# Attention logits with the high query part multiplied into both key parts at once, kept in the outputs' PSUM banks, and softmax weights normalized by ScalarE

## The chip, the cores and the metric

One core of one Trainium2 chip runs the whole program. The metric is device time in microseconds (us) of one execution. The kernel before takes 2760.2 us (median of 3 runs, 2759.58 to 2760.26).

## The reference

The program is a two-layer decoder trunk on 256 tokens of width 2048, all in float32. Layer 0 is retention plus an MLP plus a gated per-layer embedding; layer 1 is block-sparse attention plus the same two. One attention block holds 256 keys, so with 256 tokens every query sees only its own block, causally, and the attention of layer 1 is plain causal softmax attention of 16 heads of width 128 with a relative-position bias:

```
l = einsum('hqd,hkd->hqk', q, k) * dh ** -0.5
l = where(dist >= 0, l + bias[:, bucket(dist)], NEG_INF)
p = softmax(l, axis=-1)
out = einsum('hqk,hkd->hqd', p, v) @ w_o
```

Keys and values come from the normalized stream after layer 0.

## The kernel before

**Arithmetic.** Every float32 operand is cut into a high part (a cast to fp32r on ScalarE, line 221) and a low part (the difference, on VectorE, line 222), and a product is the sum of three matmuls: high by high, high by low, low by high. This goes for weights and activations alike.

**Units.** All weights are streamed as units of 128x1024. A list of units is worked off in order by `run` (line 105): for unit i it issues the load of a pair of units (line 93, on SyncE's queue), splits unit i+3 into `wh` and `wl` (`conv`, line 96; `LOOK` is 3 and there are 4 buffers of each), issues unit i's matmuls, and then runs the tasks that were registered for i. So the order of the instructions on each engine is the order in which this loop writes them; nothing is rearranged later.

**Attention.** The 16 heads are worked in four groups of four (`attention`, line 709). A group has 24 units: 8 for the keys (`ak`), 8 for the queries (`aq`, two per head), 8 for the values (`av`). In a key or query unit TensorE does 8 matmuls of 512 columns (line 155) and 8 of 256 (line 153); in a value unit 12 of 512 (lines 195 to 197). With b the group's first unit, the tasks are:

- after the second query unit of head j (b+9+2j): the two halves of the query's PSUM bank are added (`fold`: ScalarE line 226, VectorE line 227) into `qt`; one unit later `qt` is split into high and low part, `qx` (lines 221 and 222, lines 746 to 752).
- `logits(j)` at b+11+2j (line 757): six matmuls into one bank of the tag `aux` (2 banks), per head: for the first 128 queries against 128 keys, then for the second 128 queries against 256 keys. Then VectorE scales and adds the bias table (line 773), takes the row maximum (line 774), ScalarE does the exponential with the row sum (line 775), VectorE takes the reciprocal (line 776) and multiplies the weights by it (line 779).
- `turn(j)` at b+15+2j: three transposes of the weights (line 786), split into `ph_` and `pl_`.
- `values(j)` at b+25+j//2, in the next group's first units: the weights times the values, in a bank of the tag `y` (2 banks), split into the outputs `o`.

So between the logits of head j and those of head j+1 lie two units, and on VectorE the order is: logits work of head j, `wl` of one unit, low part of `qx` of head j+1, `wl` of the next unit, `fold` of head j+2, logits work of head j+1.

Of the kernel before, what the change touches and what calls it, by code (L numbers as in the profile page):

```python
# [13 lines left out]
AF = mybir.ActivationFunctionType  # L14
ALU = mybir.AluOpType
AX = mybir.AxisListType

P = 128
S = 256
# [51 lines left out]
class Core:  # L71
# [637 lines left out]
    def attention(self):  # L709
        nc = self.nc  # L710
        mm = nc.tensor.matmul
        first = len(self.units)
        self.at(first + 4, self.stats_a)
        self.at(first + 6, self.stats_b)
        sc = {}

        def q_scale():
            sc["s"] = self.cp.tile([P, 2], F32, name="qs")
            nc.vector.tensor_scalar_mul(sc["s"], self.rn, DH ** -0.5)
        self.at(first + 8, q_scale)  # L720
        self.ot = {}
        for g in range(AH // GH):
            b, st = len(self.units), {}

            def table(st=st, g=g):
                st["T"] = []
                bv = self.io["bvec"]
                for j in range(0, GH, 2):
                    t = self.slot("T", (P, 2, S))
                    for q in range(0, P, BR):  # L730
                        src = bass.AP(tensor=bv.tensor, offset=bv.offset + (g * GH + j) * BR * 384 + 127 - q, ap=[[383, BR], [BR * 384, 2], [1, S]])
                        nc.sync.dma_start(t[q:q + BR], src)
                    st["T"] += [t[:, 0], t[:, 1]]
            self.at(b, table)

            def evac_k(n, ps, st=st):
                t = self.small("kt")
                self.fold(t, ps)
                yield
                yield  # L740
                nc.vector.tensor_mul(t, t, self.rb)
                x = self.slot("kx", dt=F32R)
                self.split(x[:, :S], x[:, S:], t)
                st["k", n] = x

            def evac_q(n, ps, st=st):
                t = self.small("qt")
                self.fold(t, ps)
                yield
                x = self.slot("qx", dt=F32R)  # L750
                self.split(x[:, :S], x[:, S:], t)
                st["q", n] = x

            self.phase_a(f"ak{g}_", "att", g * 24, GH, 2, LEAD if g == 0 else 1, lambda k: self.xx[k], evac_k)
            self.phase_a(f"aq{g}_", "att", g * 24 + 8, GH, 2, 1, lambda k: self.x2[k], evac_q)

            def logits(j, st=st):
                ps = self.aux("lg")
                q, k = st["q", j], st["k", j]
                for t in range(2):  # L760
                    o = ps[:, :P] if t == 0 else ps[:, P:384]
                    n = P * (t + 1)
                    qh, ql = q[:, t * P:(t + 1) * P], q[:, S + t * P:S + (t + 1) * P]
                    mm(o, qh, k[:, :n], start=True, stop=False)
                    mm(o, qh, k[:, S:S + n], start=False, stop=False)
                    mm(o, ql, k[:, :n], start=False, stop=True)
                l = self.slot("lg", (P, 384))
                mx = self.cp.tile([P, 2], F32, name="mx", tag="mx", bufs=2)
                sm = self.cp.tile([P, 2], F32, name="sm", tag="sm", bufs=2)
                for t in range(2):  # L770
                    c = slice(0, P) if t == 0 else slice(P, 384)
                    bias = st["T"][j][:, P:] if t == 0 else st["T"][j]
                    nc.vector.scalar_tensor_tensor(l[:, c], ps[:, c], sc["s"][:, t:t + 1], bias, op0=ALU.mult, op1=ALU.add)
                    nc.vector.reduce_max(mx[:, t:t + 1], l[:, c], axis=AX.X, negate=True)
                    nc.scalar.activation(l[:, c], l[:, c], AF.Exp, bias=mx[:, t:t + 1], accum_out=sm[:, t:t + 1])
                nc.vector.reciprocal(sm, sm)
                for t in range(2):
                    c = slice(0, P) if t == 0 else slice(P, 384)
                    nc.vector.tensor_scalar_mul(l[:, c], l[:, c], sm[:, t:t + 1])
                st["p", j] = l  # L780

            def turn(j, st=st):
                p = st.pop(("p", j))
                ps = self.aux("pt")
                for i, (c, o) in enumerate(((0, 0), (1, 1), (2, 2))):
                    nc.tensor.transpose(ps[:, o * P:(o + 1) * P], p[:, c * P:(c + 1) * P], self.ident)
                h, l = self.slot("ph_", (P, 384), F32R), self.slot("pl_", (P, 384), F32R)
                self.split(h, l, ps[:, :384])
                st["t", j] = (h, l)

            def evac_v(banks, st=st):
                st["v"] = self.natural(banks, self.rn)

            def values(j, st=st, g=g):
                (vh, vl), (ph, pl) = st["v"], st["t", j]
                ps = self.bank("y", "y", 2)
                c = slice(j * P, (j + 1) * P)
                for t in range(2):
                    o = ps[:, :S] if t == 0 else ps[:, P:S]
                    p = slice(0, S) if t == 0 else slice(S, 384)  # L800
                    mm(o, vh[t][:, c], ph[:, p], start=t == 0, stop=False)
                    mm(o, vh[t][:, c], pl[:, p], start=False, stop=False)
                    mm(o, vl[t][:, c], ph[:, p], start=False, stop=t == 1)
                x = self.slot(f"o{g}_{j}", dt=F32R)
                self.split(x[:, :S], x[:, S:], ps[:, :S])
                self.ot[g * GH + j] = x

            self.phase_b(f"av{g}_", "att", g * 24 + 16, KD // 2, lambda k: self.xx[k], evac_v)
            for j in range(GH):
                self.at(b + 11 + 2 * j, lambda j=j, f=logits: f(j))  # L810
                self.at(b + 15 + 2 * j, lambda j=j, f=turn: f(j))
                self.at(b + 25 + j // 2, lambda j=j, f=values: f(j))

        self.project("att_o", "att_o", 0, KD // 2, lambda k: self.ot[k], self.add([G_MLP1]))
# [82 lines left out]
```

## Time and profile before

| | |
|---|---|
| median of 3 runs | 2760.2 us |
| profiled execution, its own time | 2760.45 us |
| span of the profiled execution | 2758.6 us |
| TensorE busy | 2745.0 us, 13776 matmuls |
| VectorE busy | 1687.8 us |
| ScalarE busy | 1316.7 us |
| granted TensorE clock | 0.999 of full speed |
| HBM traffic | 189 GB/s over the span |

The span is what the trace covers; the execution's own time is 1.85 us longer. The durations below are from this one execution. A matmul's start is observed and its end is modelled, so the distance between starts is what a matmul takes of TensorE.

### The profile page before, as it was taken

The page shows a single profiled execution, that of the slowest core. Times are in us where ns is not written, and L with a number is a line of the kernel's source. Part 1 is how long each engine was busy: PE and PEld are TensorE (multiplying, and loading weights), DVE is VectorE, ACT ScalarE, POOL GpSimd, SP SyncE. Part 2 cuts the span into 40 slices and gives each one's busy share as a digit, 9 for nine tenths or more (in the row PEclk, how much of TensorE's full clock was granted, in tenths as well). Part 3 has the DMA queues.
Part 4 walks back from the last instruction along what each step waited for, and adds up shares of the span by engine and source line. Part 5 has one row for each costly group of instructions (what it writes and reads, how often), then busy time and mean ns, then how long its engine had stood idle before and what let it go on. Part 6 is the DMA issues. An engine that isn't in the chain of part 4 may idle for free.

```text
span 2758.6 us, 34142 instructions
## 1 busy us (share of the span) xinstructions
PE 2745.0 (100%) x13776; PEld 2336.5 (85%) x13776; DVE 1687.8 (61%) x2289; ACT 1316.7 (48%) x1812; POOL 0.2 (0%) x4
## 2 busy tenths in 40 slices
PE   9999999999999999999999999999999999999998
PEld 7888888888888888888888888888888888888886
DVE  6766666655576545665546766665666446664555
ACT  6444444444454433554446555555544334544454
POOL 0000000000000000000000000000000000000000
PEclk9999999999999999999999999999999999999999
DMA  7455555555555555555565555554555555555554
GB/s 278 176 186 186 186 186 186 186 183 189 185 191 190 192 198 188 194 184 197 185 201 193 179 187 179 176 183 177 189 187 195 193 190 196 185 191 190 186 200 153
DMA packets 79451, 522.50 MB, mean 189 GB/s; under 512 B 8987, under 2 KB 12988, under 8 KB 17596
## 3 DMA queue, kind: packets, MB, share of 16 engines
q1 hardware_dynamic: 78476, 519.20, 52.7%
q10 hardware_dynamic: 816, 1.11, 0.3%
q8 instruction: 108, 1.77, 0.3%
q14 instruction: 51, 0.42, 0.0%
HBM read 517.39 MB, written 2.88 MB: 189 GB/s over the span
## 4 chain that ended last, share of the span: by engine, by line
PE 99%; DMA 0%; DVE 0%; ACT 0%; issue 0%; SPq 0%
PE up L155 17%; PE up L153 9%; PE qk L155 4%; PE ak L155 2%; PE aq L155 2%; PE qk L153 2%; PE ak L153 1%; PE aq L153 1%; PE pu L573 1%; PE xt L255 1%; PE y L461 1%; PE qk L182 0%; PE dn__11046 L195 0%; PE dn__11047 L196 0%; PE dn__21304 L197 0%; PE dn__20701 L196 0%
## 5 line engine op out<-in xcount | busy, mean ns | idle before, releaser
L222 DVE TENSOR_TENSOR wl<-raw,wh 128x1024 fp32r<-128x1024 f32 (+1 forms) x971 | 1180.0, 1221 | 656.8 <-ACT wh L221 643.8
L221 ACT CAST wh<-raw 128x1024 fp32r<-128x1024 f32 (+1 forms) x971 | 1014.9, 1050 | 714.0 <-DVE rs_y L278 29.2
L155 PE MATMUL up<-x,wh 128*128 128x512 f32 x2048 | 490.5, 391 | 0.0
L155 PEld LDWEIGHTS up<-x,wh 128*128 128x128 f32 x2048 | 376.0, 188 | 72.5
L153 PEld LDWEIGHTS up<-x,wl 128*128 128x128 f32 x2048 | 263.4, 191 | 10.4
L153 PE MATMUL up<-x,wl 128*128 128x256 f32 x2048 | 266.6, 283 | 0.0
L226 ACT COPY t<-up 128x256 f32<-128x256 f32 x128 | 47.7, 373 | 331.7 <-PE up L155 331.7
L227 DVE TENSOR_TENSOR t<-t,up 128x256 f32<-128x256 f32 x128 | 53.9, 421 | 217.0 <-ACT t L226 216.9
L155 PE MATMUL qk<-x,wh 128*128 128x512 f32 x448 | 109.9, 392 | 0.0
L155 PEld LDWEIGHTS qk<-x,wh 128*128 128x128 f32 x448 | 81.8, 188 | 15.5
L233 ACT ACTIVATE x<-xt,g 128x256 fp32r<-128x256 f32 x112 | 52.6, 479 | 51.1 <-DVE x L234 39.5
L234 DVE SCALAR_TENSOR_TENSOR x<-xt,g,x 128x256 fp32r<-128x256 f32 x112 | 53.0, 481 | 26.2 <-ACT x L233 26.0
L155 PE MATMUL aq<-x,wh 128*128 128x512 f32 x256 | 63.2, 391 | 0.0
L155 PE MATMUL ak<-x,wh 128*128 128x512 f32 x256 | 63.1, 392 | 0.0
L153 PEld LDWEIGHTS qk<-x,wl 128*128 128x128 f32 x448 | 57.4, 191 | 2.2
L153 PE MATMUL qk<-x,wl 128*128 128x256 f32 x448 | 58.1, 283 | 0.0
L533 DVE SCALAR_TENSOR_TENSOR s<-t 128x256 f32<-128x256 f32 x128 | 54.3, 425 | 4.4
L155 PEld LDWEIGHTS ak<-x,wh 128*128 128x128 f32 x256 | 46.6, 188 | 8.8
L155 PEld LDWEIGHTS aq<-x,wh 128*128 128x128 f32 x256 | 46.5, 188 | 8.7
L222 DVE TENSOR_TENSOR a<-s,a 128x256 fp32r<-128x256 f32 x128 | 53.6, 419 | 0.0
L221 ACT CAST a<-s 128x256 fp32r<-128x256 f32 x128 | 52.1, 407 | 0.0
L242 ACT ACTIVATE sq<-h 128x512 f32<-128x512 f32 x48 | 30.1, 628 | 37.4 <-DVE h L542 15.6
(1011 smaller groups left out, 4991.4 us busy)
## 6 DMA issues: line engine op xcount, KB each, us to landing
raw<-mlp_up SPq DMA_DIRECT2D x128, 1024.0 KB, 4.8
raw<-mlp_dn SPq DMA_DIRECT2D x128, 1024.0 KB, 4.8
raw<-ret_in SPq DMA_DIRECT2D x94, 1024.0 KB, 4.8
raw<-att SPq DMA_DIRECT2D x48, 1024.0 KB, 4.8
raw<-ret_out SPq DMA_DIRECT2D x32, 1024.0 KB, 4.7
raw<-ple_gate SPq DMA_DIRECT2D x32, 1024.0 KB, 4.8
raw<-att_o SPq DMA_DIRECT2D x16, 1024.0 KB, 4.8
raw<-ple_up SPq DMA_DIRECT2D x4, 1024.0 KB, 4.8
```

What stands on the lines that cost most here:

```text
L153: mm(ps[:, S:], wl[:, c], rhs[k][:, :S], start=False, stop=end)
L155: mm(ps, wh[:, c], rhs[k], start=first and k == 0, stop=end)
L221: self.nc.scalar.copy(dst_h, src)
L222: self.nc.vector.tensor_sub(dst_l, src, dst_h.bitcast(F32))
L226: self.nc.scalar.copy(dst, ps[:, :S])
L227: self.nc.vector.tensor_add(dst, dst, ps[:, S:])
L233: self.nc.scalar.activation(t[:, :S], src, AF.Copy, scale=gs)
L234: self.nc.vector.scalar_tensor_tensor(t[:, S:], src, gs, t[:, :S].bitcast(F32), op0=ALU.mult, op1=ALU.subtract)
L242: self.nc.scalar.activation(self.slot("sq"), self.h[c][:, t], AF.Square, accum_out=self.ssq[:, t, c:c + 1])
L255: self.nc.tensor.transpose(ps[:, o * P:(o + 1) * P], self.h[c][:, t, f * P:(f + 1) * P], self.ident)
L461: mm(ys[t], a, w, start=i == 0, stop=i == len(ops) - 1)
L533: nc.vector.scalar_tensor_tensor(s, t, 0.0, t, op0=ALU.max, op1=ALU.mult)
```

## The change

Three things change, all in `logits`:

- Per 128 queries there are two matmuls instead of three. The high part of the queries is multiplied with the high and the low part of the keys side by side, in one matmul of 256 columns (first 128 queries) or 512 (second 128 queries); the low part of the queries is then added onto the first half. The two halves are not summed in PSUM any more.
- The results lie in two banks of the tag `y`, one per 128 queries, instead of one bank of the tag `aux`.
- VectorE scales and adds twice per 128 queries: the first half with the bias, then the second half onto that. The multiplication of the weights by the reciprocal row sum moves from VectorE to ScalarE.

```diff
             def logits(j, st=st):
-                ps = self.aux("lg")
                 q, k = st["q", j], st["k", j]
-                for t in range(2):
-                    o = ps[:, :P] if t == 0 else ps[:, P:384]
-                    n = P * (t + 1)
+                pss = []
+                for t in range(2):
+                    ps, n = self.bank("lg", "y", 2), P * (t + 1)
                     qh, ql = q[:, t * P:(t + 1) * P], q[:, S + t * P:S + (t + 1) * P]
-                    mm(o, qh, k[:, :n], start=True, stop=False)
-                    mm(o, qh, k[:, S:S + n], start=False, stop=False)
-                    mm(o, ql, k[:, :n], start=False, stop=True)
+                    x = k if t else k.rearrange("p (a s) -> p a s", a=2)[:, :, :P]
+                    o = ps if t else ps[:, :S].rearrange("p (a s) -> p a s", a=2)
+                    mm(o, qh, x, start=True, stop=False)
+                    mm(ps[:, :n], ql, k[:, :n], start=False, stop=True)
+                    pss.append((ps[:, :n], ps[:, n:2 * n]))
...
-                    nc.vector.scalar_tensor_tensor(l[:, c], ps[:, c], sc["s"][:, t:t + 1], bias, op0=ALU.mult, op1=ALU.add)
+                    for half, rest in zip(pss[t], (bias, l[:, c])):
+                        nc.vector.scalar_tensor_tensor(l[:, c], half, sc["s"][:, t:t + 1], rest, op0=ALU.mult, op1=ALU.add)
                     nc.vector.reduce_max(mx[:, t:t + 1], l[:, c], axis=AX.X, negate=True)
                     nc.scalar.activation(l[:, c], l[:, c], AF.Exp, bias=mx[:, t:t + 1], accum_out=sm[:, t:t + 1])
                 nc.vector.reciprocal(sm, sm)
                 for t in range(2):
                     c = slice(0, P) if t == 0 else slice(P, 384)
-                    nc.vector.tensor_scalar_mul(l[:, c], l[:, c], sm[:, t:t + 1])
+                    nc.scalar.activation(l[:, c], l[:, c], AF.Copy, scale=sm[:, t:t + 1])
                 st["p", j] = l
```

On ScalarE, in the first group between the logits of head 0 and those of head 1, there stood (`lg` are the weights, `wh` a unit's high part, `qx` head 1's split query):

```order
L775 ACTIVATE lg,sm<-lg,mx 128x256
L221 CAST wh_12884<-raw_12758 128x1024
L221 CAST qx<-qt 128x256
L221 CAST wh_12908<-raw_12814 128x1024
L226 COPY qt<-aq_2_12888 128x256
L775 ACTIVATE lg,sm<-lg,mx 128x128
```

and now there stands, with lines 775 and 779 become 777 and 781:

```order
L777 ACTIVATE lg,sm<-lg,mx 128x256
L781 ACTIVATE lg<-lg,sm 128x128
L781 ACTIVATE lg<-lg,sm 128x256
L221 CAST wh_12885<-raw_12758 128x1024
L221 CAST qx<-qt 128x256
L221 CAST wh_12909<-raw_12814 128x1024
L226 COPY qt<-aq_2_12889 128x256
L777 ACTIVATE lg,sm<-lg,mx 128x128
```

Two instructions that read VectorE's reciprocal now stand between the exponential and the next unit's cast.

On VectorE, from the logits of head 1 in the first group to the following low parts (`sm` holds the row sums), there stood:

```order
L773 SCALAR_TENSOR_TENSOR lg<-lg,qs,T 128x128
L774 TENSOR_REDUCE mx<-lg 128x1
L773 SCALAR_TENSOR_TENSOR lg<-lg,qs,T 128x256
L774 TENSOR_REDUCE mx<-lg 128x1
L776 RECIPROCAL sm<-sm 128x2
L779 TENSOR_SCALAR lg<-lg,sm 128x128
L779 TENSOR_SCALAR lg<-lg,sm 128x256
L222 TENSOR_TENSOR wl_12953<-raw_12814,wh_12952 128x1024
L222 TENSOR_TENSOR qx<-qt,qx 128x256
```

and now there stands:

```order
L775 SCALAR_TENSOR_TENSOR lg<-lg,qs,T 128x128
L775 SCALAR_TENSOR_TENSOR lg<-lg,qs 128x128
L776 TENSOR_REDUCE mx<-lg 128x1
L775 SCALAR_TENSOR_TENSOR lg<-lg,qs,T 128x256
L775 SCALAR_TENSOR_TENSOR lg<-lg,qs 128x256
L776 TENSOR_REDUCE mx<-lg 128x1
L778 RECIPROCAL sm<-sm 128x2
L222 TENSOR_TENSOR wl_12955<-raw_12814,wh_12954 128x1024
L222 TENSOR_TENSOR qx<-qt,qx 128x256
```

Two additions came ahead of the maxima, two multiplications behind the reciprocal went, and the unit's low part with head 2's `qx` stands right behind the reciprocal.

## Rows read from the trace of the kernel before

**Rows 1.** The page: busy us and share by engine; the chain by engine.
```profile
PE 2745.0 (100%) x13776; PEld 2336.5 (85%) x13776; DVE 1687.8 (61%) x2289; ACT 1316.7 (48%) x1812; POOL 0.2 (0%) x4
...
PE 99%; DMA 0%; DVE 0%; ACT 0%; issue 0%; SPq 0%
```

**Rows 2.** All waits of TensorE: line, releaser, us in total, times, longest.
```profile
PE warm L364 <- DVE zero L357: 1.5, 1, 1.5
PE qk L182 <- ACT wh L221: 0.9, 2, 0.7
```

**Rows 3.** Windows, attention stage: stretch, length, busy us of PE, PEld, DVE, ACT, POOL, clock, DMA.
```profile
1590.00:1850.00 260.00, 260.00 (x1446) 226.23 (x1445) 180.52 (x302) 138.53 (x242) 0.00 (x0) 1.00 0.51 180
```

**Rows 4.** Timeline of TensorE, second group: start us, us, instruction.
```profile
1670.55 0.22 PE L764 MATMUL lg<-kx,qx 128*128 128x128 f32 x1
1670.71 0.27 PE L766 MATMUL lg<-kx,qx 128*128 128x128 f32 x1
1671.23 2.00 PE L155 MATMUL aq<-x,wh 128*128 128x512 f32 x8
...
1677.33 0.28 PE L766 MATMUL lg<-kx,qx 128*128 128x128 f32 x1
...
1683.81 0.28 PE L766 MATMUL lg<-kx,qx 128*128 128x128 f32 x1
```

**Rows 5.** Timeline of VectorE, second group, head 0 to head 1.
```profile
1665.21 0.34 DVE L773 SCALAR_TENSOR_TENSOR lg<-lg,qs,T 128x128 f32<-128x128 f32 x1
1665.59 0.29 DVE L774 TENSOR_REDUCE mx<-lg 128x1 f32<-128x128 f32 x1
1665.79 0.47 DVE L773 SCALAR_TENSOR_TENSOR lg<-lg,qs,T 128x256 f32<-128x256 f32 x1
1666.30 0.42 DVE L774 TENSOR_REDUCE mx<-lg 128x1 f32<-128x256 f32 x1
1667.39 0.17 DVE L776 RECIPROCAL sm<-sm 128x2 f32<-128x2 f32 x1 [0.67 <-ACT lg L775]
1667.59 0.55 DVE L779 TENSOR_SCALAR lg<-lg,sm 128x128 f32<-128x128 f32 x2
1668.33 1.23 DVE L222 TENSOR_TENSOR wl<-raw,wh 128x1024 fp32r<-128x1024 f32 x1 [0.19 <-ACT wh L221]
1669.47 0.42 DVE L222 TENSOR_TENSOR qx<-qt,qx 128x256 fp32r<-128x256 f32 x1
1669.81 1.22 DVE L222 TENSOR_TENSOR wl<-raw,wh 128x1024 fp32r<-128x1024 f32 x1
1671.15 0.42 DVE L227 TENSOR_TENSOR qt<-qt,aq 128x256 f32<-128x256 f32 x1
1671.49 0.34 DVE L773 SCALAR_TENSOR_TENSOR lg<-lg,qs,T 128x128 f32<-128x128 f32 x1
...
1677.87 0.56 DVE L222 TENSOR_TENSOR pl__13704<-pt,ph__13703 128x384 fp32r<-128x384 f32 x1
1678.35 0.34 DVE L773 SCALAR_TENSOR_TENSOR lg<-lg,qs,T 128x128 f32<-128x128 f32 x1
```

**Rows 6.** Timeline of ScalarE beside it.
```profile
1665.91 0.40 ACT L775 ACTIVATE lg<-lg,mx 128x128 f32<-128x128 f32 x1 [1.07 <-DVE mx L774]
...
1666.75 0.51 ACT L775 ACTIVATE lg<-lg,mx 128x256 f32<-128x256 f32 x1 [0.35 <-DVE mx L774]
1667.17 0.19 ACT L775 ACTIVATION_READ_ACCUMULATOR lg<-lg,mx 128x1 f32 x1
1667.26 1.03 ACT L221 CAST wh<-raw 128x1024 fp32r<-128x1024 f32 x1
1668.20 0.40 ACT L221 CAST qx<-qt 128x256 fp32r<-128x256 f32 x1
```

**Rows 7.** First group: head 0's first addition, head 3's low-query matmul.
```profile
1592.47 0.35 DVE L773 SCALAR_TENSOR_TENSOR lg<-lg,qs,T 128x128 f32<-128x128 f32 x1
...
1610.52 0.28 PE L766 MATMUL lg<-kx,qx 128*128 128x128 f32 x1
```

## Prediction

> **What bounds the kernel now.** I read the page's busy shares and chain first. TensorE is busy 2745.0 us of the span and holds 99% of the chain; VectorE and ScalarE stand at 61% and 48% [rows 1]. The list of TensorE's waits is complete with two entries, 1.5 and 0.9 us, both on tiles of the program's start [rows 2]. So in the attention TensorE never waits, and the windows say it again: 260 of 260 us busy from 1590 to 1850 at a granted clock of 1.00 [rows 3]. There VectorE is busy 180.52 us, 69%, more than its average. A change in this stage can win only what it takes off TensorE; it loses if something that TensorE needs comes later than it does now. The question is how much later it may come.
>
> That is read from the timelines of the three engines side by side. In the second group the low-query matmul of head 1 starts at 1670.71 [rows 4]. It needs the low part of head 1's query, which VectorE starts at 1669.47 and has after 0.42, at 1669.89 [rows 5]. The slack is 0.82 us. In a share of busy time this does not show: VectorE has free time, but this one result stands behind the whole softmax of head 0 and a 1.23 us weight split in a queue that is worked in order.
>
> **The change part by part.**
>
> TensorE. Six matmuls per head become four. Six take 1670.55 to 1671.23, 0.68 us, 0.11 each [rows 4]. I give four 0.57: the wide one of 512 columns counts two. That is 0.11 us per head, at most 1.8 us for 16. The two banks of the tag `y` cost nothing in waits: their last readers are VectorE's additions two units earlier, or the output splits eight units earlier.
>
> VectorE and ScalarE between one head's logits and the next head's query. Let S be the start of the first addition, 1665.21 in the second group [rows 5]. The path before, from the rows: S+0.38 maximum, S+0.58 second addition, S+1.09 second maximum (0.42 long), S+1.54 second exponential, read-out of its sums until 1667.36 (S+2.15), reciprocal S+2.18 to S+2.35, multiplications until 1668.14, then 0.19 wait for ScalarE's cast, weight low part at S+3.12, query low part S+4.26 to S+4.68 [rows 5, 6]. Note that the cast of the next weights starts at 1667.26, right behind the exponential and before the reciprocal; it runs beside it.
>
> After, step by step:
> - Each addition is doubled, and the second reads what the first wrote, as the maximum does now. The distances are 0.38 (1665.21 to 1665.59) and 0.51 (1665.79 to 1666.30) [rows 5]. That is +0.89 for everything behind: the reciprocal ends at S+3.24.
> - ScalarE's two normalizations need the reciprocal (+0.03, the usual gap between the engines in these rows). The trace has no such copy of this size. The nearest rows are the exponentials, same operands in size and place: 0.40 and 0.51 long, of which 0.09 overlaps the next instruction (1666.75 to 1667.17) [rows 6], so 0.31 and 0.42, together 0.73. Below: a plain cast of 256 is 0.40 long [rows 6], 0.11 under the exponential; for both sizes about 0.2 less. At the extreme they cost nothing. Above: 0.91, without overlap.
> - The cast of the next unit, 1.03 long, stands behind them in ScalarE's queue [the order shown above], and VectorE's low part needs it. So: 3.24+0.03+0.73+1.03+0.04 = S+5.07 for the weight low part, where it was S+3.12. The multiplications that left VectorE give nothing back: the cast ended after them already.
> - From there as before: 1.14 to the query's low part, 0.42 long, 0.03 to TensorE: ready at S+6.66. Then 0.34, the next weight low part 1.14, the fold 0.34 (1671.15 to 1671.49), and the next head's additions start at S+8.03 [rows 5]. For the pair head 1 to head 2 the low part of the transposed weights comes in between, 0.48 (1677.87 to 1678.35): 8.51.
>
> Before, this loop took 6.28 us (1665.21 to 1671.49) and kept up with TensorE. After, it takes 8.03 and 8.51 against TensorE's 6.5 to 6.6 (1670.71 to 1677.33 to 1683.81 [rows 4]), and TensorE has to wait three times per group, for heads 1, 2 and 3:
> - head 1: ready at 1665.21+6.66 = 1671.87, used before at 1670.71: 1.16 later.
> - head 2: additions of head 1 at 1673.24, ready at 1679.90; used before at 1677.33 [rows 4]: 2.57 later.
> - head 3: additions of head 2 at 1681.75, ready at 1688.41; used before at 1683.81 [rows 4]: 4.60 later.
>
> Behind head 3 no query is left in the group, VectorE catches up during the value and key units, and the next group starts with the same lead; groups three and four stand as group two does. The first group starts its additions later, at 1592.47: 1592.47+23.20 (8.03+8.51+6.66) = 1615.67 against 1610.52 [rows 7], 5.15. The time from the first group's to the last group's end is then longer by 3 x 4.60 + 5.15 = 18.95. Behind a waiting matmul stands all else of TensorE's queue, the next unit first, so each wait goes into the time in full. SyncE's loads wait for weight buffers that VectorE frees later by as much; their readers are later too, so nothing is added there. TensorE's own 0.11 per head is inside these waits and is not gained in heads 1 to 3; head 0's cannot be gained either, since TensorE only arrives earlier at the wait.
>
> Profiled execution 2760.45 + 18.95 = 2779.4. It lies 0.25 above the median of the runs shown; against that median I predict 2779.2.
>
> [...]
>
> **The rivals.**
>
> 1. The wait stays hidden, not slower. Mechanism: the casts get past the two normalizations on ScalarE, so that only VectorE's own work counts: weight low part at S+3.27 instead of S+3.12, query ready at S+4.86, 0.15 later than now, inside the slack of 0.82. Then 16 x 0.11 = 1.8 us are gained: 2758.7. It decides at an added delay of about 0.7 us per head. For it: the casts do not depend on the softmax. Against it: before 1666.75 ScalarE sat idle 0.35 us waiting for the maximum, with the same kind of cast next in its queue, and did not start it [rows 6]. [...]
>
> 2. Half the delay. If the second addition overlapped the first, or the copies cost nothing, the loop is shorter by 0.73 to 0.89, twelve times over four groups (three loops each): 18.95 less 8.8 to 10.7, so 2768.7 to 2770.6. For it: no row has these instructions. Against: the second addition's dependence is that of the maximum, which waits out the full 0.38.
>
> 3. The lag reaches the weights too. Behind head 3 the additions start at 1681.75+8.17 = 1689.92, and the weight low part that follows is done at 1689.92+5.07+1.23 = 1696.2; TensorE wants it some 9 us after 1688.41, at about 1697.4 (nearly 6.48 for logits, two units and a transpose [rows 4], and some 2.8 for a third unit). 1.2 us of room. If the loop were 0.4 us longer than worked out, every group would pay up to 1 us more: 2784 with the longer loop's own 12 x 0.2.
>
> [...]
>
> **How the numbers follow.** Forecast 0.76, rival 1 0.09, rival 2 0.06, rival 3 0.05, rival 4 0.04. The forecast's own range is 2774 to 2783: twelve loops times the copies' bounds, -0.2 and +0.18, and a little for the gaps. The range that is to hold 8 in 10 reaches down towards rival 2 and up to rival 3: 2770 to 2784. What this kernel can tell from no change is about 0.2%, 5.5 us. Slower by more than that: forecast, rivals 2, 3 and 4, nearly whole: 0.90. Within: rival 1 and a little of rival 2: 0.08. Faster by more: 0.02, for no case above reaches it.
>
> **What would show it.** In the profile after, the list of TensorE's waits has a new main entry: the low-query matmul of the logits waiting for VectorE's query low part, 12 times, some 15 to 20 us in all, and none for head 0. VectorE's wait for ScalarE's cast behind the logits grows from 0.19 to some 1.8 us, ScalarE's normalizations wait 0.2 to 0.3 for the reciprocal, and the first additions of two heads stand 8.0 and 8.5 us apart instead of 6.3 and 6.9. The window from 1590 is about 19 us longer, all else is not. I am wrong if TensorE shows no wait in the attention (rival 1), if the loop is 7.2 us (rival 2), or if the granted clock there is under 0.95 (rival 4).

## The result and the profile after

The changed kernel takes 2780.96 us (median of 4 runs, 2779.38 to 2781.04) against 2760.23 for the kernel before (4 runs): a ratio of 1.0073 with a 95% interval of 1.0061 to 1.0084. It is slower by 20.7 us. The profiled execution is the one of 2779.38, with a span of 2777.6 us, 19.0 us longer than before.

The list of TensorE's waits, which had two entries at the program's start [rows 2], now begins with the attention logits (line, releaser, us in total, times, longest):

```profile
PE lg L766 <- DVE qx L222: 10.9, 12, 0.9
PE lg L765 <- ACT qx L221: 3.0, 5, 0.7
PE warm L364 <- DVE zero L357: 1.5, 1, 1.5
```

Two more entries, 1.0 us in all, are at the program's start. Twelve times, three heads in each of four groups, the low-query matmul (line 766 in both kernels) waits for VectorE's low part of the query; five times (head 3 of every group and head 1 of the first) the high-query matmul ahead of it already waits for ScalarE's high part. The entries give 13.9 us, less than the 19.0 that are missing, because a matmul counts as busy until its modelled end: the idle time begins only there (of the 1.30 us between two starts shown below, 0.91 is listed). Distances of starts tell the whole. From a unit of the keys that both kernels work alike (line 155, start 1562.40 before and 1562.52 after) to the first matmul of the output projection (`att_o`, line 195, start 1847.98 and 1867.03) it is 285.58 us before and 304.51 after, 18.93 more. This distance is called the stage below.

The windows, with the columns of [rows 3], show where the time went. After, the attention stands in 279 us, and all that follows it in 908:

```profile
1590.00:1869.00 279.00, 264.82 (x1414) 224.41 (x1413) 182.89 (x302) 149.45 (x274) 0.00 (x0) 1.00 0.48 168
...
1869.00:2777.00 908.00, 897.65 (x4481) 763.88 (x4479) 526.96 (x663) 422.63 (x558) 0.00 (x0) 1.00 0.53 187
```

Before, what follows it was as long:

```profile
1850.00:2758.00 908.00, 897.61 (x4480) 763.88 (x4478) 526.80 (x663) 422.69 (x558) 0.00 (x0) 1.00 0.52 187
```

Against [rows 3] the window of the attention needs 19 us more and TensorE has 14 us idle in it; VectorE is busy 182.89 us, hardly more than the 180.52 of before, ScalarE 149.45 instead of 138.53, and the granted clock is 1.00. Neither got anywhere near full (66% and 54% of the 279 us).

VectorE's timeline in the second group, head 0's logits to head 1's, answers to [rows 5]:

```profile
1670.46 0.34 DVE L775 SCALAR_TENSOR_TENSOR lg<-lg,qs,T 128x128 f32<-128x128 f32 x1
1670.84 0.35 DVE L775 SCALAR_TENSOR_TENSOR lg<-lg,qs 128x128 f32<-128x128 f32 x1
1671.22 0.28 DVE L776 TENSOR_REDUCE mx<-lg 128x1 f32<-128x128 f32 x1
1671.43 0.47 DVE L775 SCALAR_TENSOR_TENSOR lg<-lg,qs,T 128x256 f32<-128x256 f32 x1
1671.94 0.48 DVE L775 SCALAR_TENSOR_TENSOR lg<-lg,qs 128x256 f32<-128x256 f32 x1
1672.45 0.42 DVE L776 TENSOR_REDUCE mx<-lg 128x1 f32<-128x256 f32 x1
1673.55 0.17 DVE L778 RECIPROCAL sm<-sm 128x2 f32<-128x2 f32 x1 [0.67 <-ACT lg L777]
1675.52 1.22 DVE L222 TENSOR_TENSOR wl<-raw,wh 128x1024 fp32r<-128x1024 f32 x1 [1.81 <-ACT wh L221]
1676.66 0.42 DVE L222 TENSOR_TENSOR qx<-qt,qx 128x256 fp32r<-128x256 f32 x1
...
1678.46 0.35 DVE L775 SCALAR_TENSOR_TENSOR lg<-lg,qs,T 128x128 f32<-128x128 f32 x1
...
1686.93 0.34 DVE L775 SCALAR_TENSOR_TENSOR lg<-lg,qs,T 128x128 f32<-128x128 f32 x1
```

The weight low part starts 5.06 us after the first addition (3.12 before), and VectorE idles 1.81 us for it. From head to head it takes 8.00 and 8.47 us, where it took 6.28 and 6.86.

ScalarE's timeline beside it, which answers to [rows 6]:

```profile
1672.91 0.51 ACT L777 ACTIVATE lg<-lg,mx 128x256 f32<-128x256 f32 x1 [0.87 <-DVE mx L776]
1673.33 0.19 ACT L777 ACTIVATION_READ_ACCUMULATOR lg<-lg,mx 128x1 f32 x1
1673.74 0.80 ACT L781 ACTIVATE lg<-lg,sm 128x128 f32<-128x128 f32 x2 [0.23 <-DVE sm L778]
1674.45 1.04 ACT L221 CAST wh<-raw 128x1024 fp32r<-128x1024 f32 x1
1675.39 0.40 ACT L221 CAST qx<-qt 128x256 fp32r<-128x256 f32 x1
```

The cast used to follow the exponential's read-out at once, 0.09 us behind its start [rows 6]; now it starts 1.12 us behind that start, after a wait of 0.23 for the reciprocal and two normalizations (0.71 from the first's start to the cast's).

TensorE in the same place, which answers to [rows 4]:

```profile
1675.84 0.38 PE L765 MATMUL lg<-kx,qx 128*128 128x256 f32 x1
1677.14 0.33 PE L766 MATMUL lg<-kx,qx 128*128 128x128 f32 x1 [0.91 <-DVE qx L222]
1677.30 0.45 PE L765 MATMUL lg<-kx,qx 128*128 128x512 f32 x1
1677.59 0.28 PE L766 MATMUL lg<-kx,qx 128*128 128x256 f32 x1
```

The low-query matmul starts 1.30 us after the one ahead of it; unhindered, that distance is 0.11 (below). It starts 0.06 us after the query's low part ends at 1677.08.

### The profile page after: what moved, and what is told of

It is laid out like the page before. It is cut to its first block, busy times and chain, and to the rows that moved or that the text cites. A ratio compares the mean times of both kernels' runs of the same rounds, so it can differ in the third digit from the quotient of the medians.

```text
span 2777.6 us, 34105 instructions
## 1 busy us (share of the span) xinstructions
PE 2750.0 (99%) x13744; PEld 2334.5 (84%) x13744; DVE 1690.1 (61%) x2289; ACT 1327.0 (48%) x1844; POOL 0.2 (0%) x4
## 4 chain that ended last, share of the span: by engine, by line
PE 95%; DVE 3%; ACT 1%; issue 1%; DMA 0%; SPq 0%
PE up L155 17%; PE up L153 9%; PE qk L155 4%; PE ak L155 2%; PE qk L153 2%; PE ak L153 1%; PE aq L155 1%; PE pu L573 1%; DVE lg L775 1%; PE xt L255 1%; DVE wl L222 1%; PE y L461 1%; ACT wh L221 1%; PE aq L153 0%; PE qk L182 0%
```

## The experiments

The first theory is that of the prediction, the **queue theory**: the head-to-head loop through VectorE and ScalarE became longer than TensorE's, by the doubled additions (0.89 us) and by the cast that stands behind the normalizations (1.06 us). Rivals: the merged matmuls or their banks are slower in themselves; the work moved to ScalarE costs wherever it stands; the parts simply add up. In two sets of runs, the kernel before took 2760.67 us (first four experiments, 23 runs) and 2760.51 (last four, 26 runs); each ratio is against the kernel before of its own set. The changed kernel was not run again in these sets: where a result is set against it, that is its 2780.96, 20.7 over its own kernel before. The letter S stands for the start of a head's first addition on VectorE.

**Normalization back on VectorE.** The changed kernel with

```diff
-                    nc.scalar.activation(l[:, c], l[:, c], AF.Copy, scale=sm[:, t:t + 1])
+                    nc.vector.tensor_scalar_mul(l[:, c], l[:, c], sm[:, t:t + 1])
```

> The changed kernel, with the multiplication by the reciprocal back on VectorE; the doubled additions and the merged matmuls stay. Queue theory: the next weight cast runs beside the reciprocal again, so only the additions' 0.89 us delay the next head's query: weight low part at S+4.01, query low part ready at S+5.60, loop 6.97 (7.45 with the transposed weights' split between). Per group 1.0 to 1.4 us of waiting, first group 0.5 more: 5 to 6.5 us over the kernel before, 2765 to 2767. Rival (the parts add up, half each): 2770. Rival (the matmuls or banks are slower in themselves): about 2780, as the changed kernel.

Measured: 2767.19 us, ratio 1.0024 (1.0014 to 1.0033), 6.5 us over the kernel before, the upper end of what was expected (the time itself is 0.2 above its range). VectorE's loop in the second group:

```profile
1667.86 0.34 DVE L775 SCALAR_TENSOR_TENSOR lg<-lg,qs,T 128x128 f32<-128x128 f32 x1
1671.88 1.23 DVE L222 TENSOR_TENSOR wl<-raw,wh 128x1024 fp32r<-128x1024 f32 x1 [0.18 <-ACT wh L221]
...
1674.83 0.34 DVE L775 SCALAR_TENSOR_TENSOR lg<-lg,qs,T 128x128 f32<-128x128 f32 x1
```

The weight low part comes at S+4.02 and the loop is 6.97, as worked out. The wait for the cast is back at 0.18. With the doubled additions kept, putting the normalization back on VectorE takes away two thirds of the loss.

**Only the normalization on ScalarE.** The kernel before with

```diff
-                    nc.vector.tensor_scalar_mul(l[:, c], l[:, c], sm[:, t:t + 1])
+                    nc.scalar.activation(l[:, c], l[:, c], AF.Copy, scale=sm[:, t:t + 1])
```

> The kernel before, with only the multiplication by the reciprocal moved to ScalarE; six matmuls, one addition. Queue theory: the cast waits behind reciprocal and copies, weight low part at S+4.18 instead of S+3.12, loop 7.14 and 7.62: 1.9 us per group, 2.5 in the first, 8.3 in all: 2768 to 2769. It costs more than the doubled additions although VectorE gets work taken off. Rival (ScalarE's queue lets the cast pass): 2760, no change. Rival (parts add up): about 2770, and this and the run with the normalization on VectorE together make 19; by the queue theory they make about 14, since each has to use up the same slack of 0.8 us per group first.

Measured: 2768.88 us, ratio 1.0030 (1.0018 to 1.0041), 8.2 us more. The loop, VectorE, second group:

```profile
1667.33 0.35 DVE L773 SCALAR_TENSOR_TENSOR lg<-lg,qs,T 128x128 f32<-128x128 f32 x1
1671.48 1.23 DVE L222 TENSOR_TENSOR wl<-raw,wh 128x1024 fp32r<-128x1024 f32 x1 [1.81 <-ACT wh L221]
...
1674.43 0.34 DVE L773 SCALAR_TENSOR_TENSOR lg<-lg,qs,T 128x128 f32<-128x128 f32 x1
```

S+4.15 and 7.10, against 4.18 and 7.14 expected. Taking work off VectorE alone makes this kernel slower. This run and the last together make 14.7 us, not the whole (14.67 against 18.93 in the stage): the parts do not add up, because each alone has the same slack of 0.82 us to use up first (here the low-query matmul waits 9 times, in the changed kernel 12).

**Normalization issued one unit later.** The changed kernel; the same instructions on every engine, with the two normalizations as a task of their own:

```diff
-                for t in range(2):
-                    c = slice(0, P) if t == 0 else slice(P, 384)
-                    nc.scalar.activation(l[:, c], l[:, c], AF.Copy, scale=sm[:, t:t + 1])
                 st["p", j] = l
+                st["sm", j] = sm
+
+            def norm(j, st=st):
+                l, sm = st["p", j], st["sm", j]
+                for t in range(2):
+                    c = slice(0, P) if t == 0 else slice(P, 384)
+                    nc.scalar.activation(l[:, c], l[:, c], AF.Copy, scale=sm[:, t:t + 1])
...
                 self.at(b + 11 + 2 * j, lambda j=j, f=logits: f(j))
+                self.at(b + 12 + 2 * j, lambda j=j, f=norm: f(j))
```

> The changed kernel, with ScalarE's two normalizations issued one unit later, so that the next weight cast stands ahead of them; same instructions on every engine. Queue theory: the weight low part comes at S+4.01, but the second cast now stands behind the copies and adds about 0.5 per loop: loop 7.4 and 7.9, 2.2 us per group: 2768 to 2771, half of the loss back by position alone. Rival (ScalarE's work or its port costs, wherever it stands): 2780.

Measured: 2770.77 us, ratio 1.0036 (1.0023 to 1.0050), 10.1 us over the kernel before and 10.2 under the changed one. ScalarE, second group:

```profile
1671.00 0.19 ACT L777 ACTIVATION_READ_ACCUMULATOR lg<-lg,mx 128x1 f32 x1
1671.10 1.03 ACT L221 CAST wh<-raw 128x1024 fp32r<-128x1024 f32 x1
1672.03 0.80 ACT L786 ACTIVATE lg<-lg,sm 128x128 f32<-128x128 f32 x2
1672.74 0.39 ACT L221 CAST qx<-qt 128x256 fp32r<-128x256 f32 x1
1673.03 1.04 ACT L221 CAST wh<-raw 128x1024 fp32r<-128x1024 f32 x1
```

The cast follows the read-out at once again (0.10 us behind its start), and half of the loss is gone with no instruction less. What is left is the doubled additions and the second cast, now behind the copies: the loop takes 7.45 and 7.91 us, where 7.4 and 7.9 were expected. The casts of the query stand behind the copies too, and TensorE's main wait is now for the query's high part:

```profile
PE lg L765 <- ACT qx L221: 3.9, 8, 0.8
PE lg L766 <- DVE qx L222: 1.9, 9, 0.2
```

**One addition, VectorE normalizes.** The changed kernel; it leaves out the addition of the second half, so the product of the high query part and the low key part is computed and dropped:

```diff
-                    for half, rest in zip(pss[t], (bias, l[:, c])):
+                    for half, rest in zip(pss[t][:1], (bias,)):
...
-                    nc.scalar.activation(l[:, c], l[:, c], AF.Copy, scale=sm[:, t:t + 1])
+                    nc.vector.tensor_scalar_mul(l[:, c], l[:, c], sm[:, t:t + 1])
```

> Leaves out the second addition (the product of the high query part with the low key part is computed and dropped) and normalizes on VectorE: of the change only the merged matmuls in the outputs' banks are left. Queue theory: the loop is that of the kernel before, TensorE never waits in the attention, and 16 x 0.11 to 0.15 us are gained: 2757.8 to 2758.8. Rival (a matmul of 512 columns or two banks cost TensorE as much as six matmuls): 2760.2. Rival (the merged matmuls cause the loss): over 2765.

Measured: 2759.13 us, ratio 0.9994 (0.9985 to 1.0003), 1.5 us under the kernel before and 0.3 above the expected range; the interval does not tell it from no change. TensorE's waits have no entry in the attention, and a head's logits there read:

```profile
1670.63 0.28 PE L765 MATMUL lg<-kx,qx 128*128 128x256 f32 x1
1670.74 0.22 PE L766 MATMUL lg<-kx,qx 128*128 128x128 f32 x1
1670.81 0.45 PE L765 MATMUL lg<-kx,qx 128*128 128x512 f32 x1
1671.09 0.28 PE L766 MATMUL lg<-kx,qx 128*128 128x256 f32 x1
1671.21 2.00 PE L155 MATMUL aq<-x,wh 128*128 128x512 f32 x8
```

Four matmuls take 0.58 us (1670.63 to 1671.21), where six took 0.68 [rows 4]. The stage is 1.76 us shorter than before (1562.97 to 1846.79, 283.82), which is 16 x 0.11: in the trace the gain is there. The merged matmuls are not the loss.

**Normalization on ScalarE, one addition.** The changed kernel without the second addition (the same part left out), normalization as changed:

```diff
-                    for half, rest in zip(pss[t], (bias, l[:, c])):
+                    for half, rest in zip(pss[t][:1], (bias,)):
```

> Leaves out the second addition; merged matmuls, two banks and the normalization on ScalarE stay. Queue theory: the loop is that of the run with only the normalization moved, 7.14 and 7.62, and it bounds; the matmuls' gain is inside TensorE's waits and only shows where there is none: 2767.5 to 2769, within 1 us of that run (2768.9). Rival (the matmuls' gain counts in full): 2767.1, 1.8 less.

Measured: 2768.66 us, ratio 1.0029 (1.0018 to 1.0041). With six matmuls it was 2768.88. The difference of 0.2 is nearer to none than to 1.8, though the runs of either kernel scatter by over 1 us. The traces tell more. The stage is 293.61 us (1562.34 to 1855.95), and 293.66 with six matmuls (1562.09 to 1855.75). The shorter logits fall into TensorE's waits, which grow. Their list here:

```profile
PE lg L766 <- DVE qx L222: 6.4, 12, 0.9
```

The same entry in the run with only the normalization moved:

```profile
PE lg L766 <- DVE qx L222: 5.1, 9, 0.9
```

**Banks only.** The kernel before with its six matmuls in two banks of the outputs' tag:

```diff
-                ps = self.aux("lg")
+                pss = [self.bank("lg", "y", 2) for _ in range(2)]
...
-                    o = ps[:, :P] if t == 0 else ps[:, P:384]
                     n = P * (t + 1)
+                    o = pss[t][:, :n]
...
-                    nc.vector.scalar_tensor_tensor(l[:, c], ps[:, c], sc["s"][:, t:t + 1], bias, op0=ALU.mult, op1=ALU.add)
+                    nc.vector.scalar_tensor_tensor(l[:, c], pss[t][:, :P * (t + 1)], sc["s"][:, t:t + 1], bias, op0=ALU.mult, op1=ALU.add)
```

> The kernel before, with the logits' six matmuls written into two banks of the outputs' tag instead of one of the other tag; nothing else. Queue theory: no instruction waits longer, 2760.0 to 2761.0, the same as before. Rival (the banks are the cause, by a wait on the outputs' splits or by sharing): over 2763.

Measured: 2760.47 us against 2760.51, ratio 0.9999 (0.9990 to 1.0008). The stage is 285.58 us, as before. The banks cost nothing.

**Logits one unit later.** The changed kernel; the logits are registered when the next head's query is, so that they stand behind its split:

```diff
-                self.at(b + 11 + 2 * j, lambda j=j, f=logits: f(j))
+                self.at(b + 11 + 2 * j, lambda j=j, f=logits, i=b + 12 + 2 * j: self.at(i, lambda: f(j)))
```

> The changed kernel with the logits one unit later, and nothing else. Queue theory: the query wait goes, but the loop stays at 8.0 and 8.5 us, lags by 1.7 to 2 per head, some 5 to 6 us over a group, and that is more than the weights' lead holds: TensorE now waits for weight parts late in the value units, 2 to 3 us per group: 2766 to 2772. Rival (only the query's place matters): 2758.5.

Measured: 2768.79 us, ratio 1.0030 (1.0019 to 1.0041), 8.3 us over the kernel before. The query wait is gone and another has come. Of TensorE's waits:

```profile
PE av__13719 L196 <- DVE wl L222: 0.8, 1, 0.8
...
PE av__13015 L195 <- ACT wh L221: 0.5, 1, 0.5
```

In the value units TensorE now waits for the weights' low and high parts. They do so once in each group. Moving the consumer takes away more than half of the loss, because the weights' lead (a unit is split three units ahead of its use) now carries a part of the lag; the rest is felt at the weights. VectorE's loop is 8.02 and 8.47 us, as in the changed kernel, against TensorE's 6.48 before (head 2 to head 3) [rows 4].

**Logits one unit later and normalization on VectorE.** Both edits, the doubled additions kept, nothing left out:

```diff
-                    nc.scalar.activation(l[:, c], l[:, c], AF.Copy, scale=sm[:, t:t + 1])
+                    nc.vector.tensor_scalar_mul(l[:, c], l[:, c], sm[:, t:t + 1])
...
-                self.at(b + 11 + 2 * j, lambda j=j, f=logits: f(j))
+                self.at(b + 11 + 2 * j, lambda j=j, f=logits, i=b + 12 + 2 * j: self.at(i, lambda: f(j)))
```

> The changed kernel with the normalization on VectorE and the logits one unit later, so that the next head's query is split before them; all else, the doubled additions too, as changed. Queue theory: the query is ready a whole unit before it is used, the loop of 6.97 to 7.45 us lags TensorE's 6.2 to 6.5 by 0.8 to 0.9 per head, 2.6 us over a group, which the weights' lead of 3 units takes: no wait, and the matmuls' gain stays: 2758 to 2759.5. Rival (the doubled additions cost TensorE time in themselves, through PSUM reads): about 2766, as with the logits in their place.

Measured: 2758.90 us (11 runs, 2758.50 to 2759.71), ratio to the kernel before 0.9994 (0.9986 to 1.0003). It beats the changed kernel clearly; against the one before it is 1.6 us lower, the size that was worked out for the matmuls, but inside what the interval allows for no change. The stage of the profiled execution is 283.84 us (1563.03 to 1846.87), 1.74 less than before and within 0.02 of the run with one addition; so the doubled additions cost TensorE nothing in themselves. VectorE's loop here is 6.98 us and still longer than TensorE's 6.48 (1673.27 to 1679.75, the next two heads' first high-query matmuls), but now only the weights' lead has to carry its lag, and it does:

```profile
1667.50 0.35 DVE L775 SCALAR_TENSOR_TENSOR lg<-lg,qs,T 128x128 f32<-128x128 f32 x1
...
1674.48 0.34 DVE L775 SCALAR_TENSOR_TENSOR lg<-lg,qs,T 128x128 f32<-128x128 f32 x1
```

TensorE's list of waits has only start entries again.

## Why the prediction was right

**The bound and the slack.** Reading the attention as a stage in which TensorE never waits, and then asking how late each thing that it needs may come, was the step that decided. The slack of 0.82 us under the query's low part was the right one: all twelve main waits are on it.

**The additions.** Taken as 0.38 and 0.51 us each; measured 0.38 and 0.51 from one start to the next (1670.46 to 1670.84, 1671.43 to 1671.94). The second addition starts 0.04 us after the first has ended, for both sizes (1670.80 and 1671.90): it waits for it, as assumed.

**The normalizations.** Taken as 0.73 by the exponentials; measured 0.71 until the cast starts. That the cast stands behind them cost more than their length, since it waits for the reciprocal as well (0.23 us).

**The loop.** 8.03 and 8.51 worked out, 8.00 and 8.47 measured; weight low part S+5.07 against S+5.06. The sum of 18.95 stands against 19.0 in the spans and 18.93 in the stage, and 2779.4 against 2779.38 in the profiled execution. That the mechanism was right is shown by the loop and the waits; an agreement to 0.02 us is luck, for each loop came out 0.03 to 0.04 shorter than worked out, and the runs scatter by more. The other three runs of the changed kernel lie 1.5 to 1.7 above the profiled one, so the median is 1.8 over the 2779.2 that were worked out for it; what differs between these executions is open.

**What was off.** I expected TensorE's list of waits to show 15 to 20 us in one entry. It shows 10.9 there and 3.0 in an entry that I had not named, the high part's five waits; the sizes are smaller because of the modelled ends. The first high-query matmul needs ScalarE's cast of the query, which stands behind the same cast of the weights. The output splits lie at least nine units ahead of the next group's first logits, not eight as the prediction says; the run with the banks only shows that nothing hangs on it.

**The rivals.** That the casts get past the normalizations is refuted twice: by ScalarE's timeline after, and by the run that moved the normalizations behind the cast and won 10.2 us. The half delay needed a loop of about 7.2 us; it is 8.00 (8.47 from head 1 to head 2), and loops of 6.97 to 7.45 stand only in the runs with one part undone or moved. The lag did not reach the weights, but it did in the run with the logits one unit later, so this rival's mechanism is real, and the room of 1.2 us was enough. Its time of 2784 does not come out of its terms: a loop longer by 0.4 us makes 12 x 0.4 = 4.8 us, 2784.0 by itself, and 1 us more in each of four groups would be 2788. Rival 4, at a chance of 0.04, is a lower granted clock in the attention; no run shows one. The clock was 1.00 in that window before, after and in every experiment.

## What to carry to other kernels

An engine at 66% busy (VectorE, 182.89 of 279 us) can still be the bound of a stage: what counted here is the loop through the queues of VectorE and ScalarE, from one head's work to the next result that TensorE needs (8.00 and 8.47 us), against TensorE's own time for the same loop (6.62 and 6.48 before) [rows 4]. Before moving an instruction to the less busy engine, look at what stands behind it in that engine's queue and what it waits for; here two copies, 0.71 us together, and their wait of 0.23 delayed a weight cast that had nothing to do with them. A saving on the engine that was the bound was worth next to nothing while another loop was longer and its lag was felt (0.05 of 1.76 us came through in the stage), and the parts of this change did not add up (14.67 against 18.93 us): each uses up the same slack.

## What the runs showed of the hardware

Nothing was out of line with the rows of before: the copy of 128 rows with a scale from a tile, which no row had shown, takes 0.40 us for 128 columns and 0.49 for 256, and the second of a pair overlaps the next instruction by 0.09 (0.80 long for both, 0.71 to the cast), like the exponentials. Waits of TensorE of 0.9 us of listed idle time and less, two of them close after one another in some heads, left its granted clock at 1.00. Exponentials and copies by turns brought no further load of an activation table: ScalarE has four `ACT_TABLE_LOAD`s of 1.28 us before and four after, one of them in the attention (1591.42 and 1591.54).
